# Layer 1's scores of both maps in one five-bank PSUM region

## The chip, the cores and the metric

The kernel runs on one core of a Trainium2 chip. The metric is the time of the whole program on the device, in microseconds (us), as the median of several executions; smaller is better. A profile is one further execution, recorded by the hardware, from which spans of single instructions are read. The engines named are TensorE (PE; its weight loads stand as PEld), VectorE (DVE), ScalarE (ACT), GpSimd (POOL) and SyncE (SP, which only issues DMAs here).

## What is computed

The reference is a two-layer transformer over 1024 latent tokens and 256 context tokens, width 1024. Layer 0 is a multi-head latent attention, layer 1 a differential attention with 8 heads; both end in a gated output projection and a layer norm. The change is in layer 1, which for each head does this (context tokens are keys only, since no later layer needs their output):

```python
# per head h: two maps m of 64-wide queries and keys, one 128-wide value
s1 = q1 @ k1.T * scale          # (1024, 1280): 1024 latent and 256 context keys
s2 = q2 @ k2.T * scale
o  = softmax(s1) @ v - lam * (softmax(s2) @ v)
o  = rms_norm(o, g_sub) * (1 - lambda_init) * silu(gate)
```

Everything is float32 in the reference. The kernel keeps that accuracy by splitting each operand into a high and a low float16 part and adding three products (high x high, high x low, low x high).

## The kernel before

**Steps.** Layer 1 runs over 8 heads and, in each, over 8 tiles of 128 queries: 64 steps. `step1` (L1345) issues one step. In the text below a tile's work is spread over three steps: scores and softmax in step t, the turn of its weights in step t+1, its product with the values in step t+2.

- *Scores* (`scores1`, L1135): for map 0 and 1, matmuls against 1280 keys, two each (L1144 and L1145, high and low query), in pieces of at most 512 columns. Before, every piece goes to a PSUM bank of its own from a rotation of eight: first the 256 context columns of both maps in one bank, then two banks of 512 a map. DVE takes the negated maximum of each bank (L1157, L1161) and combines them (L1163); ACT takes the exponential of each piece and its sum (L1167). After both maps DVE adds the sums up (L1170), inverts them (L1171), forms the factor of map 2 (L1172) and joins the maps (L1173: `p0 + factor * p1`, 1280 wide, from SBUF).
- *Turn* (`turn1`, L1176): PE transposes the joined weights, ten blocks of 128 x 128 (L1180), in groups of 4, 4 and 2, each group in a bank; `split16` (L179) writes the high part with ACT (L181) and the low part with DVE (L182), once a group.
- *Values* (`values1`, L1184): 30 matmuls (L1188 to L1190) into one bank; ACT scales the result out (L1193) and squares it (L1194), POOL makes the norm's factor (L159, L160) and applies it (L1201), and a DMA writes it to `o_d`.
- *Side work*: the projections of the next head's keys, queries, values and gate (`prod_k1`, `prod_q1`, `prod_v1`), and the preparation of their weights (`prod_w`). Projections are matmuls of three products (`mm3`, L185 to L187) over eight blocks of the inner dimension, and come in pieces of 512 columns (keys, queries) or 256 columns (value and gate). Keys and queries get a rotary embedding: DVE shuffles and multiplies (L1048, L1049), POOL multiplies and adds (L1050, L1051), then `split16` writes `kH` and `kL`. Values and gate are copied out by ACT (L1122, L1124), split into `vh` and `vl`, and the gate gets a SiLU (L1129). `prod_w` squares the loaded weights (L979, ACT), makes a scale from them (L982 to L989, PE, DVE and POOL) and splits them into `wH` and `wL`.

**What sets the order.** PE's order is written out by hand: within the loop over heads PE executes in the order in which the program calls it. The orders of ACT, DVE, POOL and SP are set by the framework's scheduler when the program is built, and each engine then works through its list in order. The framework also puts in the waits between engines, from the tiles that instructions write and read. How much side work PE does between the parts of a step is set by `SLOT1`, five numbers in units of PE columns: after map 0's scores (and, before, all of its exponentials are issued), after map 1's scores and the values, and after each group of the turn. In the last head there is no next projection; there the side work is the output projection (`out_tile1`, fp32 matmuls) and the transposes of its input (`out_turn`, L1262), by `SLOTO`.

```python
SLOT1 = 2900, 2900, 2900, 2900, 2900
SLOTO = 0, 7000, 7000, 7000, 7000
```

PSUM has eight banks of 512 fp32 columns. From L1006 on, all eight rotate under one tag (`bank("b")`): scores, turns, values, projections and output.

Of the kernel before, what the change touches and what calls it, by code (L numbers as in the profile page):

```python
# [9 lines left out]
F32 = mybir.dt.float32  # L10
# [3 lines left out]
AF = mybir.ActivationFunctionType  # L14
ALU = mybir.AluOpType
AX = mybir.AxisListType

P = 128
D = 1024
KT = D // P  # L20
SEQ = 1024
CTX = 256
NTOK = SEQ + CTX
NT = NTOK // P
# [16 lines left out]
CHUNKS = ((0, 512), (512, 512), (1024, 256))  # L41
MROW0, MROW1 = 16.0, 1024.0
PW = 16.0
SLOT1 = 2900, 2900, 2900, 2900, 2900
SLOTO = 0, 7000, 7000, 7000, 7000
SWAP16 = [(i + 16) % 32 for i in range(32)]

# [1 line left out]
def fv(ap):  # L49
    return ap.bitcast(F32)  # L50
# [3 lines left out]
def hybrid_kernel(  # L54
# [7 lines left out]
    pe, act, dve, pool, sp = nc.tensor, nc.scalar, nc.vector, nc.gpsimd, nc.sync  # L62
# [6 lines left out]
    def nm(s):  # L69
        uid[0] += 1  # L70
        return f"{s}_{uid[0]}"
# [3 lines left out]
    banks = {}  # L75
    pstack = ctx.enter_context(ExitStack())

    def set_banks(**tags):
        pstack.close()
        banks.clear()  # L80
        banks.update(tags)
        banks["pool"] = pstack.enter_context(
            tc.tile_pool(name=nm("psum"), bufs=1, space=bass.MemoryType.PSUM, reuse_waits="tile"))
# [4 lines left out]
    def bank(tag, dt=F32):  # L88
        return banks["pool"].tile([P, 512], dt, tag=tag, bufs=banks[tag], name=nm("ps_" + tag))
# [21 lines left out]
    def col(n, name, dt=F32):  # L111
        return cpool.tile([P, n], dt, tag=name, name=name)
# [21 lines left out]
    lcf = col(3, "lcf")  # L134
# [15 lines left out]
    idn = fv(idr)  # L150
# [24 lines left out]
    def split(hi, lo, src, e_hi=None, e_lo=None):  # L175
        (e_hi or act.copy)(hi, src)
        (e_lo or dve).tensor_tensor(lo, src, fv(hi), op=ALU.subtract)  # L177

    def split16(hi, lo, src, scale):  # L179

        act.activation(hi, src, AF.Copy, scale=scale)  # L181
        dve.scalar_tensor_tensor(lo, src, scale, hi, op0=ALU.mult, op1=ALU.subtract)  # L182
# [628 lines left out]
    def chain(*gs):  # L811
        for g in gs:
            yield from g
# [72 lines left out]
    with ow_ctx, spool("o0") as op0:  # L886
# [14 lines left out]
        for t in (8, 9, 0, 1, 2, 3, 4, 5, 6, 7):  # L901
# [5 lines left out]
            s = 0 if t < 8 else 1  # L907
# [7 lines left out]
            for hh in range(2):  # L915
                tb = bank("d")
# [40 lines left out]
    def w1(tag):  # L957
        sh, d, b = TAG1[tag]
        return rot(place[tag], sh, d, tag, b)
# [43 lines left out]

    for _ in prod_w(0, 0, lambda: bank("c"), act):
        pass
    set_banks(b=8)  # L1006

    sp.dma_start(cosB, cs1[0])
    sp.dma_start(sinB, cs1[1])
# [125 lines left out]
    def scores1(h, t):  # L1135

        ks = kt1[h]
        q1, qs = qt1[h]
        ts = slice(t * P, (t + 1) * P)
        mx, sm = w1("mx"), w1("sm")  # L1140
        p = [w1("p0"), w1("p1")]

        def st_of(out, m, c0, n):
            pe.matmul(out, qs[m][:, ts], ks[m][:, c0:c0 + n], start=True, stop=False)  # L1144
            pe.matmul(out, q1[m][:, ts], ks[m][:, c0:c0 + n], start=False, stop=True)  # L1145

        st = {}

        def chunk(c0, ms):
            n = 512 // len(ms)  # L1150
            st[c0, ms] = b = bank("b")
            for i, m in enumerate(ms):
                st_of(b[:, i * n:(i + 1) * n], m, c0, n)
            return b

        b = chunk(SEQ, (0, 1))
        dve.tensor_reduce(mx[:, 0:2], b.rearrange("p (a b) -> p a b", a=2), axis=AX.X, op=ALU.max, negate=True)  # L1157
        for m in range(2):
            for i, c0 in enumerate((0, 512)):
                b = chunk(c0, (m,))  # L1160
                dve.tensor_reduce(mx[:, 2 + 2 * m + i:3 + 2 * m + i], b, axis=AX.X, op=ALU.max, negate=True)  # L1161
            nb = mx[:, 6 + m:7 + m]
            dve.tensor_scalar(nb, mx[:, 2 * m + 2:2 * m + 3], mx[:, 2 * m + 3:2 * m + 4], mx[:, m:m + 1],  # L1163
                              op0=ALU.min, op1=ALU.min)
            for i, (c0, n, b) in enumerate(((0, 512, st[0, (m,)]), (512, 512, st[512, (m,)]),
                                            (SEQ, CTX, st[SEQ, (0, 1)][:, m * CTX:(m + 1) * CTX]))):
                act.activation(p[m][:, c0:c0 + n], b, AF.Exp, bias=nb,  # L1167
                               accum_out=sm[:, 2 + 3 * m + i:3 + 3 * m + i])
            yield
        dve.tensor_reduce(sm[:, 0:2], sm[:, 2:8].rearrange("p (a b) -> p a b", a=2), axis=AX.X, op=ALU.add)  # L1170
        dve.reciprocal(sm[:, 2:4], sm[:, 0:2])  # L1171
        dve.scalar_tensor_tensor(sm[:, 4:5], sm[:, 3:4], nlam, sm[:, 0:1], op0=ALU.mult, op1=ALU.mult)  # L1172
        dve.scalar_tensor_tensor(p[0], p[1], sm[:, 4:5], p[0], op0=ALU.mult, op1=ALU.add)  # L1173
        yield p[0], sm

    def turn1(pc, ph, pl, k0, n):  # L1176

        st = bank("b")
        for j in range(n):
            pe.transpose(st[:, j * P:(j + 1) * P], pc[:, (k0 + j) * P:(k0 + j + 1) * P], idn)  # L1180
        split16(ph[:, k0:k0 + n, :], pl[:, k0:k0 + n, :],
                st[:, :n * P].rearrange("p (a b) -> p a b", a=n), lcf[:, 0:1])

    def values1(h, t, ph, pl, sm):  # L1184
        vh, vl = vt[h]
# [76 lines left out]
    def out_turn(t, k0, n):  # L1262

        o, _ = og[t]
        if k0 == 0:
            oT[t] = w1("tH"), w1("tL")
        tH, tL = oT[t]
        tb = bank("b")
        for j in range(n):
            pe.transpose(tb[:, j * P:(j + 1) * P], o[:, (k0 + j) * P:(k0 + j + 1) * P], idn)  # L1270
        f = lambda x: x[:, k0:k0 + n, :].rearrange("p a b -> p (a b)")
        split(f(tH), f(tL), tb[:, :n * P])
# [65 lines left out]
    with tc.manual_schedule(engines={ENG[c] for c in MAN1}):  # L1338
        for _ in chain(weave(chain(prod_k1(0), prod_q1(0, 0), prod_q1(0, 1)), prod_w(0, 1), WAT[0]),
                       weave(prod_v1(0), prod_w(1, 0), WAT[1])):  # L1340
            while later:
                later.pop(0)()
        joined, turned = [], []

        def step1(cur, side, at):  # L1345

            with tc.high_priority(HP):
                if cur:
                    S = scores1(*cur)
                    next(S)  # L1350
            some(side, at[0])
            with tc.high_priority(HP):
                if cur:
                    next(S)
                if turned:
                    values1(*turned.pop(0))
            some(side, at[1])
            pc = None
            if joined:
                c_, pc, sm = joined.pop(0)  # L1360
                ph, pl = w1("ph"), w1("pl")
                turned.append((*c_, ph, pl, sm))
            for (k0, n), v in zip(((0, 4), (4, 4), (8, 2)), at[2:]):
                if pc is not None:
                    with tc.high_priority(HP):
                        turn1(pc, ph, pl, k0, n)
                some(side, v)
            if cur:
                with tc.high_priority(HP):
                    joined.append((cur, *next(S)))  # L1370
            for _ in range(len(later)):
                later.pop(0)()

        g1 = gate_row1()
        part = lambda: (v for _, v in zip(range(4), g1))
        for h in range(H1):
            last = h == H1 - 1
            if not last:
                G = chain(weave(weave(chain(prod_k1(h + 1), prod_q1(h + 1, 0), prod_q1(h + 1, 1)), part(), (1, 9, 17, 25)),
                                prod_w(h + 1, 1), WAT[0]),  # L1380
                          weave(prod_v1(h + 1), prod_w(h + 2, 0) if h + 2 < H1 else
                                chain(*[out_w1(k, lambda: w1("ws").rearrange("p a b -> p (a b)")) for k in range(NOW)]),
                                WAT[1] if h + 2 < H1 else range(1, 40, 4)))
            else:
                while later:
# [96 lines left out]
```

## Time and profile before

| | us |
|---|---|
| median of 3 runs | 1862.71 |
| lowest and highest run | 1861.32 and 1863.7 |
| the profiled execution (span from first to last instruction) | 1870.0 |
| PE busy in it | 1696.2 |
| DVE busy | 1245.6 |
| ACT busy | 1077.1 |
| POOL busy | 835.2 |

The profiled execution is 0.4% longer than the median of the runs. The mean clock granted to TensorE in it was 0.969 of full speed. Busy time is the union of an engine's rows; a PE row reaches from a matmul's start to the modelled end of its results, and the next matmul can start before that end. In a row of the groups, the first numbers after the bar are total busy time and mean nanoseconds of one instruction; the number after the second bar is the time for which its engine stood idle just before such an instruction, followed by what ended that idling. In a row of the waits: total us, times, longest. In a row of the timeline: start, length, engine, line, operation. In a row of the stretches: bounds, length, then busy us with counts for PE, PEld, DVE, ACT and POOL, the granted clock, the DMA share and GB/s.

Layer 1's steps run from about 1032 us to the end.

### The profile page before, as it was taken

To read this page: it belongs to the slowest core of one execution; us is meant where nothing else is said; L and a number is where in the kernel's file an instruction comes from. 1 tells how busy PE (TensorE), PEld (TensorE's weight loads), DVE (VectorE), ACT (ScalarE), POOL (GpSimd) and SP (SyncE) were. 2 spreads that over 40 slices of the span, in tenths; PEclk is the share of its full clock that TensorE was granted. 3 is DMA by queue.
4 is the path that set the end of the run, shared out by engine and by line. 5 is a ranking of instruction groups with operands and counts; after the bars stand their busy time and mean duration, and the time that the engine had idled before them with its cause. 6 is when DMAs were issued, how large, how long until landed. Compare 5 with 4: busy or idle time off the path is not lost. (4 is left out here: it accounts for less than half of the span.)

```text
span 1870.0 us, 36547 instructions
## 1 busy us (share of the span) xinstructions
PE 1696.2 (91%) x14468; PEld 1237.0 (66%) x14468; DVE 1245.6 (67%) x2072; ACT 1077.1 (58%) x2143; POOL 835.2 (45%) x741
## 2 busy tenths in 40 slices
PE   7889998999999998868979999999999999988998
PEld 3888965656666565556756576767666666666776
DVE  7546766565565657526764777787877777878674
ACT  3432047867777787711123667676767676767542
POOL 1443026767767676646662213222222222433654
PEclk9999799999999999979999999999999999999999
DMA  8245630111111113043333222222121212224341
GB/s 307 62 126 182 189 108 18 39 33 36 42 44 32 32 41 100 25 164 123 124 127 106 71 63 66 62 64 58 56 49 44 59 46 61 63 53 139 99 131 68
DMA packets 111225, 154.84 MB, mean 83 GB/s; under 512 B 13415, under 2 KB 84679, under 8 KB 111054
## 3 DMA queue, kind: packets, MB, share of 16 engines
q1 hardware_dynamic: 104238, 146.22, 26.1%
q10 hardware_dynamic: 6816, 6.29, 1.0%
q8 instruction: 114, 1.87, 0.4%
q14 instruction: 57, 0.47, 0.1%
HBM read 98.65 MB, written 27.07 MB: 67 GB/s over the span
## 5 line engine op out<-in xcount | busy, mean ns | idle before, releaser
L716 POOL TENSOR_TENSOR pl<-p,ph 128x1024 f16<-128x1024 f32 (+1 forms) x176 | 362.8, 2066 | 155.9 <-ACT ph L715 129.5
L1167 ACT ACTIVATE p<-ps_b,mx 128x512 f32<-128x512 f32 (+1 forms) x384 | 230.6, 618 | 83.1 <-DVE mx L1163 82.7
L696 DVE TENSOR_REDUCE mx<-ps_a 128x1 f32<-128x1024 f32 x128 | 155.6, 1223 | 138.2 <-PE ps_a L694 138.2
L714 ACT ACTIVATE p<-ps_a,esc 128x1024 f32<-128x1024 f32 (+1 forms) x176 | 189.2, 1075 | 100.4 <-PE ps_a L772 94.5
L715 ACT CAST ph<-p 128x1024 f16<-128x1024 f32 (+1 forms) x176 | 177.1, 1006 | 5.5
L1161 DVE TENSOR_REDUCE mx<-ps_b 128x1 f32<-128x512 f32 x256 | 165.6, 682 | 0.0
L785 PE MATMUL ps_d<-Vh,pl 128*128 128x65 f16 x1344 | 147.5, 195 | 5.2 <-POOL pl L716 5.1
L782 PE MATMUL ps_d<-Vh,ph 128*128 128x65 f16 x1344 | 149.5, 196 | 0.0
L784 PE MATMUL ps_d<-Vl,ph 128*128 128x64 f16 x1344 | 148.3, 193 | 0.0
L185 PE MATMUL ps_b<-h1H,wH 128*128 128x512 f16 (+1 forms) x384 | 133.5, 348 | 14.1 <-DVE pl L182 6.7
L185 PE MATMUL ps_b<-wH,h1H 128*128 128x256 f16 x512 | 139.5, 272 | 4.4 <-ACT p L1167 4.2
L1192 POOL TENSOR_TENSOR sm<-sm,us 128x1 f32<-128x1 f32 x64 | 18.3, 285 | 271.9 <-DVE sm L1171 258.6
L187 PE MATMUL ps_b<-wH,h1L 128*128 128x256 f16 x512 | 139.5, 273 | 0.0
L186 PE MATMUL ps_b<-wL,h1H 128*128 128x256 f16 x512 | 139.5, 272 | 0.0
L1144 PE MATMUL ps_b<-KS,QS 128*128 128x512 f16 (+1 forms) x384 | 126.1, 345 | 12.0 <-DVE pl L182 6.1
L782 PEld LDWEIGHTS <-ph 128*128 128x128 f16 x1344 | 124.2, 98 | 18.4 <-issue 5.5
L187 PE MATMUL ps_b<-h1H,wL 128*128 128x512 f16 (+1 forms) x384 | 133.2, 347 | 0.8 <-DVE wL L182 0.8
L186 PE MATMUL ps_b<-h1L,wH 128*128 128x512 f16 (+1 forms) x384 | 133.4, 347 | 0.0
L784 PEld LDWEIGHTS <-ph 128*128 128x128 f16 x1344 | 124.9, 99 | 12.4 <-issue 0.8
L770 PE MATMUL ps_a<-qH,KH 100*128 100x512 f16 x320 | 123.6, 386 | 9.7 <-ACT p L714 4.3
L1145 PE MATMUL ps_b<-KS,Q 128*128 128x512 f16 (+1 forms) x384 | 129.1, 345 | 0.0
L785 PEld LDWEIGHTS <-pl 128*128 128x128 f16 x1344 | 124.1, 98 | 6.6 <-POOL pl L716 6.5
(370 smaller groups left out, 5161.9 us busy)
## 6 DMA issues: line engine op xcount, KB each, us to landing
ws<-in_dw SPq DMA_DIRECT2D x30, 512.0 KB, 3.8
adw<-in_ada_w SPq DMA_DIRECT2D x24, 512.0 KB, 5.0
g<-sg_d SPq DMA_DIRECT2D x18, 512.0 KB, 3.7
adaw<-in_ada_w SPq DMA_DIRECT2D x16, 512.0 KB, 7.1
sg_d<-gg ACTq DMA_DIRECT2D x40, 128.0 KB, 2.8
o<-o_d SPq DMA_DIRECT2D x10, 512.0 KB, 3.5
o_d<-op SPq DMA_DIRECT2D x7, 640.0 KB, 3.7
xt<-in_xT SPq DMA_DIRECT2D x16, 256.0 KB, 3.6
```

The costliest lines, as they stand in the source:

```text
L185: pe.matmul(ps, aH, bH, start=start, stop=False, skip_group_check=skip)
L186: pe.matmul(ps, aH, bL, start=False, stop=False, skip_group_check=skip)
L187: pe.matmul(ps, aL, bH, start=False, stop=stop, skip_group_check=skip)
L696: dve.tensor_reduce(mx[:, t, 0:1], ps, axis=AX.X, op=ALU.max)
L714: act.activation(p32[:, :n], st, AF.Exp, scale=esc0)
L715: act.copy(ph[:, :n], p32[:, :n])
L716: pool.tensor_tensor(pl[:, :n], p32[:, :n], ph[:, :n], op=ALU.subtract)
L782: pe.matmul(pv[:, t, :], ph[:, ts], Vh[:, k, h, :], start=(k == kcs[0] and t == 0), stop=False, skip_group_check=True)
L784: pe.matmul(pv[:, t, :V0], ph[:, ts], Vl[:, k, h, :], start=False, stop=False, skip_group_check=True)
L785: pe.matmul(pv[:, t, :], pl[:, ts], Vh[:, k, h, :], start=False, stop=(k == NT - 1), skip_group_check=True)
L1161: dve.tensor_reduce(mx[:, 2 + 2 * m + i:3 + 2 * m + i], b, axis=AX.X, op=ALU.max, negate=True)
L1167: act.activation(p[m][:, c0:c0 + n], b, AF.Exp, bias=nb, accum_out=sm[:, 2 + 3 * m + i:3 + 3 * m + i])
```

## The change

Five of the eight banks become one tile, `spsum`, of 2 x 1280 fp32 columns, allocated once; three banks are left in the rotation. Map 0's scores stand in columns 0 to 1279 (banks 0, 1 and half of 2), map 1's in columns 1280 to 2559. Each map then has one maximum (L1157 of the changed kernel) and one exponential with its sum (L1158), both 1280 wide; the combining and adding instructions go. The first 256 columns of map 1 are computed right after map 0. The turn writes its ten transposes to columns 0 to 1279 of the same tile, in groups of 8 and 2 (L1177), and splits them with one pair of 1280-wide instructions. In the last head, the output's first seven transposes go to columns 1536 on (L1267). The slots of side work become `2900, 0, 2900, 4350, 4350`; their sum is as before. Scores are at L1145 and L1146, values at L1185 to L1187 in the changed kernel.

```diff
-SLOT1 = 2900, 2900, 2900, 2900, 2900
+SLOT1 = 2900, 0, 2900, 4350, 4350
...
-    set_banks(b=8)
+    set_banks(b=3)
+    spsum = banks["pool"].tile([P, 2 * NTOK], F32, tag="s", bufs=1, name=nm("ps_s"))
...
-        b = chunk(SEQ, (0, 1))
-        dve.tensor_reduce(mx[:, 0:2], b.rearrange("p (a b) -> p a b", a=2), axis=AX.X, op=ALU.max, negate=True)
-        for m in range(2):
-            for i, c0 in enumerate((0, 512)):
-                b = chunk(c0, (m,))
-                dve.tensor_reduce(mx[:, 2 + 2 * m + i:3 + 2 * m + i], b, axis=AX.X, op=ALU.max, negate=True)
-            nb = mx[:, 6 + m:7 + m]
-            dve.tensor_scalar(nb, mx[:, 2 * m + 2:2 * m + 3], mx[:, 2 * m + 3:2 * m + 4], mx[:, m:m + 1],
-                              op0=ALU.min, op1=ALU.min)
-            for i, (c0, n, b) in enumerate(((0, 512, st[0, (m,)]), (512, 512, st[512, (m,)]),
-                                            (SEQ, CTX, st[SEQ, (0, 1)][:, m * CTX:(m + 1) * CTX]))):
-                act.activation(p[m][:, c0:c0 + n], b, AF.Exp, bias=nb,
-                               accum_out=sm[:, 2 + 3 * m + i:3 + 3 * m + i])
-            yield
-        dve.tensor_reduce(sm[:, 0:2], sm[:, 2:8].rearrange("p (a b) -> p a b", a=2), axis=AX.X, op=ALU.add)
+        W = NTOK
+        cuts = (0, 512, 1024, W), (0, 256, 768, W)
+
+        def part(m, i):
+            c0, c1 = cuts[m][i:i + 2]
+            st_of(spsum[:, m * W + c0:m * W + c1], m, c0, c1 - c0)
+
+        def weights(m):
+            s_ = spsum[:, m * W:(m + 1) * W]
+            dve.tensor_reduce(mx[:, m:m + 1], s_, axis=AX.X, op=ALU.max, negate=True)
+            act.activation(p[m], s_, AF.Exp, bias=mx[:, m:m + 1], accum_out=sm[:, m:m + 1])
+
+        for i in range(3):
+            part(0, i)
+        part(1, 0)
+        weights(0)
+        yield
+        for i in (1, 2):
+            part(1, i)
+        weights(1)
+        yield
...
-        st = bank("b")
-        for j in range(n):
-            pe.transpose(st[:, j * P:(j + 1) * P], pc[:, (k0 + j) * P:(k0 + j + 1) * P], idn)
-        split16(ph[:, k0:k0 + n, :], pl[:, k0:k0 + n, :],
-                st[:, :n * P].rearrange("p (a b) -> p a b", a=n), lcf[:, 0:1])
+        for j in range(k0, k0 + n):
+            pe.transpose(spsum[:, j * P:(j + 1) * P], pc[:, j * P:(j + 1) * P], idn)
+        if k0 + n == NT:
+            split16(ph, pl, spsum[:, :NTOK].rearrange("p (a b) -> p a b", a=NT), lcf[:, 0:1])
...
-        tb = bank("b")
+        tb = spsum[:, 1536 + k0 * P:] if n > 1 else bank("b")
...
-            for (k0, n), v in zip(((0, 4), (4, 4), (8, 2)), at[2:]):
-                if pc is not None:
+            for (k0, n), v in zip(((0, 8), (8, 2), (NT, 0)), at[2:]):
+                if pc is not None and n:
```

More of the change, by code (lines that the diff above doesn't have):

```diff
@@ L1145, in st_of @@
             pe.matmul(out, q1[m][:, ts], ks[m][:, c0:c0 + n], start=False, stop=True)
[L1147 to L1154, printed above, removed]
-        b = chunk(SEQ, (0, 1))
-        dve.tensor_reduce(mx[:, 0:2], b.rearrange("p (a b) -> p a b", a=2), axis=AX.X, op=ALU.max, negate=True)
-        for m in range(2):
-            for i, c0 in enumerate((0, 512)):
-                b = chunk(c0, (m,))
-                dve.tensor_reduce(mx[:, 2 + 2 * m + i:3 + 2 * m + i], b, axis=AX.X, op=ALU.max, negate=True)
-            nb = mx[:, 6 + m:7 + m]
-            dve.tensor_scalar(nb, mx[:, 2 * m + 2:2 * m + 3], mx[:, 2 * m + 3:2 * m + 4], mx[:, m:m + 1],
-                              op0=ALU.min, op1=ALU.min)
-            for i, (c0, n, b) in enumerate(((0, 512, st[0, (m,)]), (512, 512, st[512, (m,)]),
-                                            (SEQ, CTX, st[SEQ, (0, 1)][:, m * CTX:(m + 1) * CTX]))):
-                act.activation(p[m][:, c0:c0 + n], b, AF.Exp, bias=nb,
-                               accum_out=sm[:, 2 + 3 * m + i:3 + 3 * m + i])
-            yield
-        dve.tensor_reduce(sm[:, 0:2], sm[:, 2:8].rearrange("p (a b) -> p a b", a=2), axis=AX.X, op=ALU.add)
+        W = NTOK
[16 more added lines that the diff above has]
+        yield
         dve.reciprocal(sm[:, 2:4], sm[:, 0:2])
```

## The prediction

> **What bounds the kernel now.** I read the page first (busy shares and the 40 slices), then the timeline of DVE for the length of a head of layer 1, the timeline of PE for what a step costs, and the waits.
>
> ```profile
> span 1870.0 us, 36547 instructions
> PE 1696.2 (91%) x14468; PEld 1237.0 (66%) x14468; DVE 1245.6 (67%) x2072; ACT 1077.1 (58%) x2143; POOL 835.2 (45%) x741
> ...
> PE   7889998999999998868979999999999999988998
> ```
>
> PE is the bound, at 9 tenths or more through nearly all of layer 1 (slices 22 to 40). The change touches layer 1 alone, so what counts is what makes PE wait there. Layer 1 goes by heads of 8 steps (one query tile each); the first reduction of a head marks its start:
>
> ```profile
> 1033.33 0.69 DVE L1157 TENSOR_REDUCE mx<-ps_b 128x2 f32<-128x512 f32 x1 [0.73 <-PE ps_b L1145]
> ...
> 1706.28 0.68 DVE L1157 TENSOR_REDUCE mx<-ps_b 128x2 f32<-128x512 f32 x1
> ```
>
> These are head 0 and head 7: (1706.28 - 1033.33) / 7 = 96.1 us a head. How much of it is PE's own work? PE overlaps its rows, so I take distances between starts.
>
> ```profile
> 1395.84 0.22 PE L1190 MATMUL ps_b<-vh,pl 128*128 128x128 f16 x1
> 1395.90 0.22 PE L1188 MATMUL ps_b<-vh,ph 128*128 128x128 f16 x1
> ...
> 1398.06 0.60 PE L1180 MATMUL ps_b<-idr,p 128*128 128x128 f32 x4
> ...
> 1404.43 0.27 PE L1144 MATMUL ps_b<-KS,QS 128*128 128x256 f16 x1
> ...
> 1404.54 0.27 PE L1145 MATMUL ps_b<-KS,Q 128*128 128x256 f16 x1
> ...
> 1404.87 0.38 PE L1144 MATMUL ps_b<-KS,QS 128*128 128x512 f16 x1
> ...
> 1405.08 0.38 PE L1145 MATMUL ps_b<-KS,Q 128*128 128x512 f16 x1
> ```
>
> 512 columns cost 0.21 us, 256 cost 0.11, a value matmul 0.055, a transpose (0.60 - 0.27) / 3 = 0.11: some 0.417 us per 1000 columns. A head has 8 x 5120 columns of scores (17.1 us), 8 x 30 value matmuls (13.2), 80 transposes (8.8) and, counted from the loops, 110,592 columns of projections (46.2): 85.3 us. So **10.8 us a head, 1.35 a step, is all that PE loses to waits today**; across seven heads a perfect change could win 76 us. The largest such wait is for the exponentials:
>
> ```profile
> PE ps_b L1180 <- ACT p L1167: 16.3, 19, 2.0
> ```
>
> That is 16.3 us in 19 waits, in the stretch of the seven heads.
>
> **The change part by part.** PE's matmuls are the same in number and size; they are only reordered. ACT and DVE get fewer, longer instructions. What decides is what PE waits for. In the changed program as built, the waits on the region `ps_s` are by the whole tile, not by the columns: map 1's second chunk (columns 1536 on) waits for map 0's exponential (columns 0 to 1279) in 64 of 64 steps; the first transpose (columns 0 on) waits for map 1's exponential in 62 of 64; map 1's maximum waits for map 0's exponential; the next step's first score waits for the low half of the split. In before, scores went to fresh banks of eight. So a step becomes one chain: scores 0, maximum, exponential, scores 1, maximum, exponential, transposes, split high, split low, next scores. PE works through it only with what its hand-written order has between.
>
> No row of before is 1280 wide from PSUM; I extend the nearest rows in a straight line.
>
> ```profile
> L1161 DVE TENSOR_REDUCE mx<-ps_b 128x1 f32<-128x512 f32 x256 | 165.6, 682 | 0.0
> L696 DVE TENSOR_REDUCE mx<-ps_a 128x1 f32<-128x1024 f32 x128 | 155.6, 1223 | 138.2 <-PE ps_a L694 138.2
> ...
> L182 DVE SCALAR_TENSOR_TENSOR pl<-ps_b,lcf,ph 128x512 f16<-128x512 f32 x128 | 90.8, 744 | 13.4 <-ACT ph L181 13.4
> ...
> L182 DVE SCALAR_TENSOR_TENSOR pl<-ps_b,lcf,ph 128x256 f16<-128x256 f32 x64 | 30.4, 476 | 1.4 <-ACT ph L181 1.4
> ```
> ```profile
> L714 ACT ACTIVATE p<-ps_a,esc 128x1024 f32<-128x1024 f32 x160 | 178.3, 1114 | 100.4 <-PE ps_a L772 94.5 <-PE ps_a L705 5.9
> L1167 ACT ACTIVATE p<-ps_b,mx 128x512 f32<-128x512 f32 x256 | 173.4, 686 | 83.1 <-DVE mx L1163 82.7
> ...
> L181 ACT ACTIVATE ph<-ps_b,lcf 128x512 f16<-128x512 f32 x128 | 88.5, 715 | 13.1 <-PE ps_b L1180 13.1
> ...
> L181 ACT ACTIVATE ph<-ps_b,lcf 128x256 f16<-128x256 f32 x64 | 32.7, 511 | 2.7 <-PE ps_b L1180 2.7
> ```
>
> Maximum: 0.682 + 768 x (1.223 - 0.682) / 512 = 1.49. Exponential: 0.686 + 768 x (1.114 - 0.686) / 512 = 1.33. Split high: 0.715 + 768 x (0.715 - 0.511) / 256 = 1.33; low: 0.744 + 768 x (0.744 - 0.476) / 256 = 1.55. Bounds: no less than the 1024-wide 1.22 and 1.11, no more than two and a half 512-wide ones, 1.71 and 1.72. The straight line is nearest. The hand-overs:
>
> ```profile
> 420.46 0.59 PE L694 MATMUL ps_a<-KH,qH 96*128 96x512 f16 x2
> ...
> 421.10 2.36 DVE L696 TENSOR_REDUCE mx<-ps_a 128x1 f32<-128x1024 f32 x2 [0.50 <-PE ps_a L694]
> ```
> ```profile
> 1409.08 0.27 DVE L1163 TENSOR_SCALAR mx<-mx 128x1 f32<-128x1 f32 x1
> ...
> 1409.38 0.69 ACT L1167 ACTIVATE p<-ps_b,mx 128x512 f32<-128x512 f32 x1 [1.05 <-DVE mx L1163]
> ```
> ```profile
> 1399.82 0.67 ACT L1167 ACTIVATE p<-ps_b,mx 128x512 f32<-128x512 f32 x1
> ...
> 1400.38 0.19 ACT L1167 ACTIVATION_READ_ACCUMULATOR p<-ps_b,mx 128x1 f32 x1
> ...
> 1400.63 0.27 PE L185 MATMUL ps_b<-wH,h1H 128*128 128x256 f16 x1 [0.34 <-ACT p L1167]
> ```
>
> PE to DVE 0.05, DVE to ACT 0.03, the accumulator read 0.08 past the exponential, ACT to PE 0.06; a matmul ends 0.16 after the next could start. Maximum and exponential together: 0.16 + 0.05 + 1.49 + 0.03 + 1.33 + 0.08 + 0.06 = **3.2 us**, twice a step.
>
> *Wait 1* (map 0): the cover is the side work at slot 2900, two pieces of 1536 columns, 1.28 us; PE stands 1.92. *Wait 2* (map 1): slot 0 gives no side work, 30 value matmuls cover 1.65; PE stands 1.55. *Wait 3* (split, 1.33 + 1.55 + 0.3 = 3.2 too): 3.2 to 3.8 us of side work covers it in seven steps, 2.56 in the eighth: 0.6 a head. A clean head: 85.3 + 8 x 3.47 + 0.6 = 113.7, that is 17.6 over today; seven heads **+123 us**.
>
> *Queues.* On ACT and DVE, whose order is fixed, other work stands ahead of a link of this chain; it now holds PE up directly.
>
> ```profile
> L181 ACT ACTIVATE wH<-ws,uw 128x1024 f16<-128x1024 f32 x30 | 32.9, 1138 | 23.4 <-DVE uw L286 23.4
> ...
> L979 ACT ACTIVATE wsq<-ws 128x1024 f32<-128x1024 f32 x27 | 29.1, 1080 | 19.2 <-DMA ws<-in_dw 19.2
> ...
> L181 ACT ACTIVATE kH<-rr,es 128x512 f16<-128x512 f32 x16 | 11.7, 732 | 32.6 <-POOL rr L1051 32.6
> L181 ACT ACTIVATE vh<-Vf,kc 128x1280 f16<-128x1280 f32 x8 | 11.3, 1407 | 0.0
> ...
> L1129 ACT ACT_TABLE_LOAD x8 | 10.3, 1283 | 0.1
> ...
> L1129 ACT ACTIVATE gg<-gg,uw 128x1024 f32<-128x1024 f32 x8 | 9.2, 1150 | 0.1
> ```
> ```profile
> L1050 POOL TENSOR_TENSOR rsw<-rsw,sinB 128x512 f32<-128x512 f32 x30 | 38.1, 1270 | 86.7 <-DVE rsw L1048 86.7
> ```
>
> From the changed order, per head, against an exponential that could start 3.0 us into its step: step 0 has vh, silu and two table loads first (1.41 + 1.15 + 2 x 1.28 = 5.1 us from 0.4 on): 2.5 late. Step 2: the maximum stands behind a scalar that waits for two rope passes on POOL (2 x 1.27) and the weight-range chain, 2.5 late, then two wH and kH ahead of map 1's exponential, 0.9. Steps 3 and 4: kH waits for the rope on POOL (3.5 us in, then 0.73), in step 3 a 1.08 square after it: 2.5 and 1.2. Step 6: two wH (1.1), two squares ahead of the split (0.9). Sum 11.6 a head, **+81 us**. Bounds: 0, if order and idle gaps hide all; 120, if each comes half again longer. ACT's saving (six exponentials and three splits become two and one) is off PE's path. So are the smaller maxima. Three banks for the rest cost nothing here: a bank's reader has finished two allocations earlier, covered by the matmuls between.
>
> *Last head.* Slot 0 is 0, so wait 1 is bare: 3.2 instead of 1.92. Slot 1 (7000 columns) covers wait 2. The output transposes now write the same tile and so wait for the split: 3.2 less 0.64 of cover, 2.6. How long such a step takes today:
>
> ```profile
> 1785.57 0.64 DVE L1157 TENSOR_REDUCE mx<-ps_b 128x2 f32<-128x512 f32 x1
> ...
> 1802.55 0.64 DVE L1157 TENSOR_REDUCE mx<-ps_b 128x2 f32<-128x512 f32 x1
> ```
>
> That is 16.98 us, against 15.95 of matmuls by the distances above: 1.0 lost. Six full steps x (3.2 + 2.6 - 1.0) is 29; with the two short first steps I take **+31**.
>
> Sum: 1870 + 123 + 81 + 31 + 10 (clock, below) = 2115 in a profiled execution. The three runs' median is 1862.71 against the 1870.0 of this one, 0.4% less: **2107 us**.
>
> **Rules weighed.** What a wait does to the clock, the trace of before shows once in full:
>
> ```profile
> 1174.35 0.44 PE L1180 MATMUL ps_b<-idr,p 128*128 128x128 f32 x2 [1.96 <-ACT p L1167]
> ```
> ```profile
> 1172.00:1176.00 4.00, 2.04 (x14) 1.38 (x13) 4.00 (x9) 2.48 (x9) 0.00 (x0) 0.93 0.48 110
> 1176.00:1180.00 4.00, 4.00 (x21) 2.49 (x20) 3.05 (x8) 3.26 (x10) 2.73 (x3) 0.65 0.46 136
> ```
>
> After 1.96 us of idling the granted clock sinks to 0.93 and 0.65 of full speed in two stretches of 4 us: 4 x 0.07 + 4 x 0.35 = 1.7 us of PE's work are lost. I charge 0.5 us for each of some 20 long waits (the late steps above), since a slow stretch falls partly into the next wait: the 10 us. The Trainium skill (TensorE: Matmul & The Clock Gate, section What's actually happening) has the gate fall to half after an idle window of about 3.4 us; the row above fell after less, and by the rule the sum would be the same, as only the late steps stand that long.
>
> **Rivals.** (a) *Clean chain*: the same waits, but the queue delays vanish into the engines' new idle time: 1870 + 123 + 31 = 2024, 2016 timed. For it: ACT and DVE lose work. Against: the order is fixed. (b) *Clock*: every step's two stands trip the gate, 1.7 us lost in each of 56 steps, +95: 2210, 2201 timed. For it: the row above; against: both stands are shorter than 2 us in a clean step. (c) *Faster, by bank*: the waits bind only where both sides touch one bank of 512 columns. Then wait 1 is gone (bank 3 against 0 to 2), and of wait 2 only the last two transposes (bank 2) wait, 0.5 us: map 1's maximum starts 4.5 us into the step, its exponential ends at 7.7, PE comes at 7.2. A head is 85.3 + 4 + 0.6 = 89.9, seven win 43: 1827, 1820 timed. It decides where the two stands together fall under today's 1.35 us a step, against 3.47 worked out. Against: the program's waits are tile-wide in every step. The Trainium skill (PSUM — Partial Sum Buffer, section PSUM bank collisions raise a hardware error) asks for guards by bank and quadrant, no wider, which is what (c) would be; no run here shows a collision. (d) The change doing nothing: excluded, the waits are in the program.
>
> **How the numbers follow.** Forecast 0.62, (a) 0.19, (b) 0.13, (c) 0.04, rest 0.02. Upper end: 2107, and 39 for the queue delays at their upper bound, and 34, half of what the 1280-wide pairs at their upper bound would add (112 x 0.61): 2180. Lower end: (a), 2016, less a fifth of what their lower bound would take off (112 x 0.49): 2005. (b), (c) and the rest stay out, 0.19. A measurement of this kernel tells about 0.2% from no change. Faster 0.04, within 0.2% 0.01, slower 0.95.
>
> **What would show it.** Right: heads of 120 to 130 us; in the waits, PE's second map (line 1145) standing for ACT's exponential some 2 us in each of 64 steps, and the transposes (1177) for it some 1.5; DVE and ACT under 60% busy in layer 1; 1280-wide rows near 1.5 and 1.3. Wrong: PE 90% busy in layer 1, waits under 1.35 us a step, or granted clock near 0.8 throughout (rival b).

## The result

The changed kernel takes **2179.09 us** (median of 4 runs, 2175.37 to 2184.89), the one before 1862.01 beside it (4 runs, 1860.17 to 1863.7): a ratio of 1.1703, 95% interval 1.168 to 1.1726. It is 317 us slower. The forecast was 2107, its range 2005 to 2180: the sign and the mechanism held. The time lies at the range's very top, and two of the four runs (2180.25 and 2184.89) lie above it.

**The profile after.** The head of the page, and its slices:

```profile
span 2173.6 us, 35376 instructions
...
PE 1778.5 (82%) x14468; PEld 1293.1 (59%) x14468; DVE 1199.3 (55%) x1560; ACT 1011.5 (47%) x1503; POOL 888.3 (41%) x741
...
PE   7989999999999869879667777777877777776777
...
PEclk9998999999999989989899899999999999998889
```

The number of matmuls is the same, 14468. DVE and ACT have lost 46 and 66 us of work, and PE, at 9 tenths through layer 1 before, is now at 6 to 8. Its busy time has grown by 82 us, though it does the same work: most of that is the granted clock, as the stretches below show. In what follows PE "stands" while it sits idle before an instruction that waits. Where did the 303.6 us between the two profiled executions arise? The stretches of layer 1, first of before, then of after: seven heads, then the last one with the end.

```profile
1033.33:1706.28 672.95, 624.80 (x5242) 451.88 (x5241) 521.61 (x1020) 460.72 (x1264) 191.21 (x311) 0.99 0.21 56
1706.28:1870.00 163.72, 142.30 (x927) 112.77 (x925) 108.29 (x197) 78.55 (x192) 82.72 (x79) 0.95 0.37 124
```
```profile
1030.25:1939.63 909.38, 683.47 (x5238) 491.86 (x5237) 479.02 (x575) 405.36 (x707) 242.79 (x311) 0.92 0.15 41
1939.63:2173.60 233.97, 168.87 (x926) 129.54 (x925) 108.49 (x130) 68.75 (x109) 87.74 (x79) 0.84 0.27 86
```

Length less PE's busy time is PE's idle time. The seven heads: 909.38 - 672.95 = 236.4 longer, of which 177.8 is idle (48.1 became 225.9) and 58.7 is busy time at a granted clock of 0.92 instead of 0.99. The last head: 70.3 longer, 43.7 idle and 26.6 busy, clock 0.84 for 0.95. So nearly three quarters of the loss is standing, the rest longer busy time. PE's waits in the seven heads name all of the standing (their sum is 225.5):

```profile
PE ps_s L1145 <- ACT p L1158: 162.9, 56, 8.7
PE ps_s L1177 <- ACT p L1158: 58.8, 48, 3.1
PE ps_s L1145 <- DVE pl L182: 3.8, 8, 0.5
```

These are the prediction's three waits: map 1's scores for map 0's exponential (wait 1), the transposes for map 1's (wait 2), the next scores for the split (wait 3). One after the other on PE's timeline they look so; the bracket holds the idle time just before the row:

```profile
1305.61 0.59 PE L1145 MATMUL ps_s<-KS,QS 128*128 128x512 f16 x1 [3.72 <-ACT p L1158]
...
1310.58 1.09 PE L1177 MATMUL ps_s<-idr,p 128*128 128x128 f32 x8 [0.88 <-ACT p L1158]
...
1321.41 0.38 PE L1145 MATMUL ps_s<-KS,QS 128*128 128x512 f16 x1 [1.74 <-ACT p L1158]
...
1325.53 1.09 PE L1177 MATMUL ps_s<-idr,p 128*128 128x128 f32 x8 [1.43 <-ACT p L1158]
...
1338.46 0.38 PE L1145 MATMUL ps_s<-KS,QS 128*128 128x512 f16 x1 [4.31 <-ACT p L1158]
```

A clean step stands for 1.74 and 1.43 us; step 0 (3.72) and step 2 (4.31) are late. What the clock makes of the matmuls behind the stands of 1.74 and 4.31 is in two stretches of 4 us that begin with them:

```profile
1321.41:1325.41 4.00, 2.69 (x34) 2.04 (x33) 1.49 (x1) 1.35 (x3) 0.00 (x0) 1.00 0.00 0
1338.46:1342.46 4.00, 4.00 (x33) 3.44 (x33) 2.75 (x3) 4.00 (x4) 0.00 (x0) 0.60 0.00 0
```

Almost the same 33 or 34 matmuls take 2.69 us at full clock behind the clean wait, and all 4 us at 0.60 behind the late one. The rows show the same behind step 0, whose first matmul takes 0.59 us for 0.38, and why wait 2 is only 0.88 there: the matmuls that cover it are slower, so PE arrives later. Part of what the clock takes falls into the next wait.

### The profile page after: what moved, and what is told of

It is laid out like the page before. It is cut to its first block, busy times and chain, and to the rows that moved or that the text cites. A ratio compares the mean times of both kernels' runs of the same rounds, so it can differ in the third digit from the quotient of the medians.

```text
span 2173.6 us, 35376 instructions
## 1 busy us (share of the span) xinstructions
PE 1778.5 (82%) x14468; PEld 1293.1 (59%) x14468; DVE 1199.3 (55%) x1560; ACT 1011.5 (47%) x1503; POOL 888.3 (41%) x741
## 4 chain that ended last, share of the span: by engine, by line
PE 48%; DVE 17%; ACT 15%; issue 7%; DMA 6%; POOL 5%; SPq 1%; DVEq 0%; POOLq 0%; ACTq 0%
PE ps_b L187 5%; PE ps_b L185 5%; ACT p L1158 5%; PE ps_b L186 5%; DVE mx L1157 5%; PE ps_s L1177 4%; PE ps_a L770 3%; PE ps_s L1145 3%; PE ps_a L771 2%; PE ps_a L772 2%; DMA ws<-in_dw 2%; PE ps_s L1146 2%; ACT ph L181 2%; PE ps_a L185 2%; DVE pl L182 2%
## 5 line engine op out<-in xcount | busy, mean ns | idle before, releaser
L1157 DVE TENSOR_REDUCE mx<-ps_s 128x1 f32<-128x1280 f32 x128 | 190.7, 1490 | 226.5 <-PE ps_s L1146 226.5
L1158 ACT ACTIVATE p<-ps_s,mx 128x1280 f32<-128x1280 f32 x128 | 169.4, 1323 | 295.8 <-DVE mx L1157 295.7
L1145 PE MATMUL ps_s<-KS,QS 128*128 128x512 f16 (+1 forms) x384 | 140.4, 374 | 203.7 <-ACT p L1158 191.5
L1146 PEld LDWEIGHTS <-Q 128*128 128x128 f16 x384 | 39.0, 102 | 250.3 <-issue 227.1
L182 DVE SCALAR_TENSOR_TENSOR pl<-ps_s,lcf,ph 128x1280 f16<-128x1280 f32 x64 | 99.2, 1550 | 131.2 <-ACT ph L181 131.2
L1185 PE MATMUL ps_b<-vh,ph 128*128 128x128 f16 x640 | 150.4, 260 | 0.0
L1186 PE MATMUL ps_b<-vl,ph 128*128 128x128 f16 x640 | 149.7, 260 | 0.0
L1187 PE MATMUL ps_b<-vh,pl 128*128 128x128 f16 x640 | 148.8, 259 | 0.0
L181 ACT ACTIVATE ph<-ps_s,lcf 128x1280 f16<-128x1280 f32 x64 | 85.0, 1329 | 133.4 <-PE ps_s L1177 133.4
L1177 PE MATMUL ps_s<-idr,p 128*128 128x128 f32 x640 | 96.9, 284 | 60.9 <-ACT p L1158 60.6
```

Source lines behind the costliest of these rows:

```text
L1157: dve.tensor_reduce(mx[:, m:m + 1], s_, axis=AX.X, op=ALU.max, negate=True)
L1158: act.activation(p[m], s_, AF.Exp, bias=mx[:, m:m + 1], accum_out=sm[:, m:m + 1])
L1177: pe.transpose(spsum[:, j * P:(j + 1) * P], pc[:, j * P:(j + 1) * P], idn)
L1185: pe.matmul(ps, ph[:, kc, :], vh[:, kc, :], start=kc == 0, stop=False)
```

## The experiments

Ratios are against runs of the kernel before on the same chip, with 95% intervals. The theory: PE stands because one tile holds both maps and the turn, so that whole-tile waits put maximum, exponential, maximum, exponential and split in one chain; queues on ACT and DVE lengthen it, and the clock adds to it. The rivals: the order of side work, the shortage of banks, or the clock alone.

**1. More cover in the same chain.** Only the slots of the changed kernel are altered.

```diff
-SLOT1 = 2900, 0, 2900, 4350, 4350
+SLOT1 = 6000, 3000, 0, 2750, 2750
```

> The changed kernel with the side work dealt out otherwise: slots 6000, 3000, 0, 2750, 2750 in place of 2900, 0, 2900, 4350, 4350. Theory (PE stands for the tile-wide waits, less what side work covers): wait 1 falls from 1.92 to 0.64 us a step, wait 2 from 1.55 to 0.3, wait 3 rises from 0 to 1.0; 1.5 us a step less, some 85 us in seven heads, and fewer falls of the clock: 2060 to 2095 us. Rival (the time is lost to work queued ahead on ACT and DVE, whatever PE does meanwhile): 2165 to 2195.

Measured: 2054.93, ratio 1.1029 (1.1002 to 1.1057), 124 us less and 5 below the theory's range. The waits of layer 1, last head included:

```profile
PE ps_s L1145 <- ACT p L1158: 97.9, 63, 7.5
PE ps_s L1145 <- DVE pl L182: 66.2, 56, 9.2
...
PE ps_s L1177 <- ACT p L1158: 8.7, 10, 1.8
```

Wait 1 is halved, wait 2 nearly gone, and wait 3 has come up in their place, since the split has 5500 columns behind it instead of 8700. The same side work hides what it stands in front of; there is too little of it for all three.

**2. A tile for each map.** Three banks each, two left for the rest; maximum, exponential and split stay 1280 wide, and the slots stay those of the changed kernel. The turn writes map 0's tile, the output's turns map 1's.

```diff
-    set_banks(b=3)
-    spsum = banks["pool"].tile([P, 2 * NTOK], F32, tag="s", bufs=1, name=nm("ps_s"))
+    set_banks(b=2)
+    smap = [banks["pool"].tile([P, 1536], F32, tag=f"s{m}", bufs=1, name=nm(f"ps_s{m}")) for m in range(2)]
...
-            s_ = spsum[:, m * W:(m + 1) * W]
+            s_ = smap[m][:, :W]
...
-            pe.transpose(spsum[:, j * P:(j + 1) * P], pc[:, j * P:(j + 1) * P], idn)
+            pe.transpose(smap[0][:, j * P:(j + 1) * P], pc[:, j * P:(j + 1) * P], idn)
```

> The changed kernel with a three-bank tile for each map, so that no wait goes across the maps; two banks are left for the rest, map 1's columns are cut 256, 512, 512 as before, and the output's eighth transpose goes to map 1's tile too. All 1280-wide instructions stay. Theory (the waits across the maps are the loss): waits 1 and 2 go in all steps, 56 x 3.47 = 194 us and 35 in the last head, and with them most of the clock's falls, some 75: 1850 to 1900 us. Rival (too few banks for the rest, or the wide instructions): with one bank fewer still, 2150 or more.

Measured: 1941.34, ratio 1.0433 (1.0396 to 1.047). Of 317 us, 238 are gone, with the wide instructions all in place; 77 us stay, more than the theory said. The run also has six banks for the maps instead of five and two for the rest instead of three, so 238 is what is left after those.

```profile
PE ps_s L1145 <- DVE pl L182: 23.3, 19, 4.0
...
PE ps_s L1177 <- ACT p L1158: 18.3, 17, 2.5
PE ps_b L185 <- ACT gg L1125: 17.0, 17, 1.2
PE ps_b L1185 <- DVE kr L1063: 10.8, 7, 1.6
```

Wait 1 is gone; waits on the rest's two banks (`ps_b`) are new, 47 us in sum. Two more runs kept these tiles and dealt the side work out anew: slots of 4000, 0, 0, 5250, 5250 and of 5000, 1500, 0, 4000, 4000.

> A tile of three banks for each map and two banks for the rest, as in the run with two tiles, and besides the slots 4000, 0, 0, 5250, 5250: more cover ahead of the transposes for map 0's exponential, the ten transposes together, 10500 columns behind the split. That run took 1941. Theory (what was left there are the waits of the transposes and of the next scores on queue delays, some 66 us in the waits, beside some 35 for the shortage of two banks): 1890 to 1920 us. Rival (the rest is the two banks, or the clock): 1935 us or more.

> Two tiles of three banks again, with the slots 5000, 1500, 0, 4000, 4000: 5.4 us of matmuls between map 0's scores and the transposes, 3.3 behind them for the split. With the slots 2900, 0, 2900, 4350, 4350 it took 1941, with 4000, 0, 0, 5250, 5250 1961. Theory (what is left are the transposes' waits for map 0's exponential, some 40 to 70 us of idling): 1900 to 1925 us. Rival (two banks for the rest are the bound, so that moved side work only moves the waits): 1935 us or more.

Measured: 1961.12, ratio 1.0522 (1.0503 to 1.0542), and 1943.19, ratio 1.0428 (1.0403 to 1.0453). Both missed the theory and lie where the rival put them, at 1935 or more. In the first, the transposes' wait for ACT's exponential grew from 18.3 to 32.5 us in spite of more cover; why is open. In the second it nearly went (3.3 us), and wait 3 grew instead:

```profile
PE ps_s L1145 <- DVE pl L182: 45.5, 29, 4.0
```

The waits on the rest's two banks were as before, 47 us in sum. The 77 us did not go with either set of slots; no run gave these two tiles a third bank for the rest.

**3. Wait 2 alone.** As in 2, but the turn goes to map 1's tile (`smap[1]` for `smap[0]` in the turn and its split).

> A tile of three banks for each map as in the run with two tiles, and the slots of the changed kernel, but the turn goes to map 1's tile instead of map 0's: the transposes wait for map 1's exponential again (wait 2), no score waits for the other map's (wait 1 gone), and the split has the next scores of map 0 and a slot of side work in front of the next writer. That run took 1941. Theory (wait 2 costs by itself: some 1.4 us a step bare in 56 steps, and queue delays of map 1's pair): 2000 to 2050 us. Rival (wait 1 is the whole loss; wait 2 only repeats it): 1935 to 1965.

Measured: 2070.67, ratio 1.1116 (1.1095 to 1.1137): 129 us more than in 2, where the theory said 60 to 110. The two runs differ in nothing but the tile that the turn writes.

```profile
PE ps_s L1177 <- ACT p L1158: 135.7, 57, 5.9
```

That is 2.4 us a step, not the clean 1.43 and not the 1.2 that wait 2 has in the changed kernel (58.8 / 48). Wait 2 by itself costs more than half of what all the waits across maps do (129 of 238), so the waits do not add up: where one is taken away, another becomes longer. That it meets the queues which wait 1 took on itself before is likely, but no run shows it alone.

**4. Single banks: five, or six, for scores and turns.** The kernel before with its 512-column pieces, its scores and turns restricted to five banks (the rest has three), then to six (the rest has two). The output's turns are among the five or six too, except in the first the eighth.

```diff
-    set_banks(b=8)
+    set_banks(s=5, b=3)
...
-            st[c0, ms] = b = bank("b")
+            st[c0, ms] = b = bank("s")
...
-        st = bank("b")
+        st = bank("s")
```

> The kernel before, with its 512-wide instructions and its order, but with the banks divided as in the change: scores, turns and output transposes rotate in five banks, all else in three. Theory (the division of the banks costs next to nothing): 1855 to 1880 us. Rival (three banks left for the rest cost a good part of the 317 us): 1920 or more.

> The kernel before with single banks of 512 columns, six of them for scores, turns and the output's turns and two for the rest (the run with five and three took 1925). Theory (that run's loss is the turn's first bank, which is that of the context scores and comes free only with map 1's last exponential; a sixth bank gives an earlier one): 1880 to 1910 us. Rival (the loss is the shortage in the rest's banks): above 1925.

Measured: 1924.89, ratio 1.0332 (1.0307 to 1.0356), and 1937.54, ratio 1.0401 (1.0382 to 1.0421). Both went against the theory and lie in the ranges of the rivals; the waits say whether for the rivals' reasons. With five and three:

```profile
PE ps_s L1180 <- ACT p L1167: 71.2, 34, 5.6
...
PE ps_b L185 <- ACT gg L1124: 6.1, 7, 0.9
```

With six and two:

```profile
PE ps_b L1120 <- ACT gg L1124: 17.4, 7, 2.5
PE ps_b L185 <- ACT gg L1124: 16.8, 9, 2.6
PE ps_s L1180 <- ACT p L1167: 16.1, 15, 2.1
PE ps_b L185 <- ACT o L1193: 13.5, 12, 1.8
...
PE ps_b L1188 <- DVE uw L286: 7.3, 6, 2.0
PE ps_b L185 <- DVE kr L1049: 5.7, 5, 1.4
```

The sixth bank does what was expected of it: the transposes' wait falls from 71.2 to 16.1, the size that it had in before. But the third bank, taken from the rest, costs as much: the five waits on `ps_b` shown come to 60.7, against the 6.1 above (with the smaller ones 69 against 8). So three banks for the rest are nearly free and two are not, and five for scores and turns, rotated in the order of the kernel before, are too few even when each bank is waited for by itself. The first run's rival had the number right and the banks wrong; the second's had both right.

**5. The order of side work alone.** The kernel before, eight banks, with the changed kernel's slots; and the other way, with 4000, 4000, 2500, 2000, 2000.

> The kernel before with only the slots of the changed one (2900, 0, 2900, 4350, 4350 for five times 2900), eight banks as before. Theory (the order of side work alone costs little while scores go to fresh banks; the waits are the region's): 1855 to 1890 us. Rival (the order alone, with no side work between map 1's scores and the transposes, is a large part of the loss): 1920 us or more.

> The kernel before with only its slots changed, to 4000, 4000, 2500, 2000, 2000: the other way from the changed kernel's slots, which alone cost 23 us. Theory (side work ahead of the transposes hides the exponentials): the waits of the transposes shrink by up to 16 us, 1848 to 1862 us. Rival (moved side work is missed behind the turn as much as it helps before it): 1863 to 1885.

Measured: 1886.32, ratio 1.012 (1.01 to 1.014), and 1864.5, ratio 1.0005 (0.9989 to 1.0021). The new order costs 23 us by itself, in the upper part of the theory's range. The other way makes no difference: that theory failed, and there is nothing to win from the slots of before.

**6. One queue.** The changed kernel without the gate's SiLU, so that ACT does not change its function table twice in step 0 of a head.

```diff
-            act.activation(g, g, AF.Silu, scale=uv)
+            act.activation(g, g, AF.Copy, scale=uv)
```

> The changed kernel with the gate's SiLU left out (a plain scaled copy stands in its place), so that ACT no longer swaps its function table twice a head in step 0; all else as after. Theory (queues on ACT ahead of the chain hold PE up): step 0's wait for map 0's exponential falls from 3.7 to about 1.7 us, 2 to 4 us a head with the clock, so 2150 to 2165 us. Rival (what stands ahead of the exponential is not what makes step 0 late): 2175 to 2185.

Measured: 2164.1, ratio 1.1617 (1.1583 to 1.1652), 15 us less. Step 0 and step 2 of the head whose steps are shown above, in this kernel:

```profile
1295.89 0.38 PE L1145 MATMUL ps_s<-KS,QS 128*128 128x512 f16 x1 [1.74 <-ACT p L1158]
...
1327.89 0.59 PE L1145 MATMUL ps_s<-KS,QS 128*128 128x512 f16 x1 [4.31 <-ACT p L1158]
```

Step 0's 3.72 has become the clean 1.74, and step 2's 4.31 has stayed. The exponentials that ended the two stands of step 0, first with the SiLU and then without:

```profile
1304.14 1.33 ACT L1158 ACTIVATE p<-ps_s,mx 128x1280 f32<-128x1280 f32 x1
```
```profile
1294.42 1.33 ACT L1158 ACTIVATE p<-ps_s,mx 128x1280 f32<-128x1280 f32 x1 [0.75 <-DVE mx L1157]
```

In both kernels PE goes on 1.47 us after this instruction starts. With the SiLU ACT came to it from a table load without a pause; without it ACT had been idle for 0.75 us and waited for the maximum. So what stands in ACT's queue ahead of the exponential holds PE up. For step 2 the trace of the changed kernel names DVE's queue: its maximum comes behind an instruction that waits for POOL.

```profile
1335.40 0.15 DVE L284 TENSOR_SCALAR uw<-uw 128x1 int32<-128x1 int32 x1 [3.02 <-POOL uw L986]
1335.47 1.48 DVE L1157 TENSOR_REDUCE mx<-ps_s 128x1 f32<-128x1280 f32 x1
```

**7. The clock.** The changed kernel with matmuls of 384 columns, into columns that nobody reads, in front of wait 1 (10, and 18 in the last head) and behind the values (8), so that PE is not seen idle.

```diff
+    def fill(h, ph, n):
+        vh = vt[h][0]
+        for _ in range(n):
+            pe.matmul(vbank[0][:, P:512], ph[:, 0, :], vh[:, 0:3, :], start=True, stop=True)
...
+            if cur and turned:
+                vbank.append(bank("b"))
+                fill(turned[0][0], turned[0][2], FILL[0] if at is SLOT1 else FILL[2])
...
+        fill(h, ph, FILL[1])
```

> The changed kernel with idle matmuls of 384 columns (0.16 us each) into unused columns of the values' bank: 10 ahead of wait 1 (18 in the last head) and 8 ahead of wait 2, so that PE works in its stands instead of idling. They add no result. Theory now (the clock's falls cost 60 to 80 us, where the prediction charged 10): they run in time that is lost anyway, the granted clock in layer 1 rises from 0.92 to over 0.97, and the time falls to 2100 to 2140 us. Rival 1 (the clock costs about 10): 2165 to 2185. Rival 2 (PE does not stand there): up by 64 x 2.9 = 185, over 2300.

Measured: 2155.2, ratio 1.1571 (1.1535 to 1.1607), 24 us less. Its seven heads:

```profile
1022.75:1918.60 895.85, 802.31 (x6212) 555.43 (x6211) 479.86 (x575) 408.80 (x707) 233.12 (x311) 0.98 0.16 42
```

The clock is up from 0.92 to 0.98 and the heads are shorter by 13.5 us: matmuls that compute nothing of use shorten the run. Neither number that was on record holds: the clock is worth more than 10 us, and removing most of its loss gained less than 60 to 80. A likely reason is that faster matmuls cover less, so that PE stands longer for the same chain; no run shows it alone. The fill can hold PE up a little itself, so 24 is more likely too low than too high.

**8. The last head.** The changed kernel with the last head's side work placed anew.

```diff
-SLOTO = 0, 7000, 7000, 7000, 7000
+SLOTO = 3500, 3500, 0, 7000, 14000
...
-        tb = spsum[:, 1536 + k0 * P:] if n > 1 else bank("b")
+        tb = spsum[:, 1536 + k0 * P:]
```

> The changed kernel with only the last head's side work placed anew (SLOTO 3500, 3500, 0, 7000, 14000 for 0, 7000, 7000, 7000, 7000; the output's eighth transpose goes to the region too): 3500 columns now lie ahead of map 1's rest, the transposes follow at once and the output's transposes come later after the split. Theory (the last head's 70 us over before are bare waits of 3.5 us for map 0's exponential, of 2.4 us for the split, and the clock that these take): the waits shrink to some 1.9 and under 1, the last head with the tail falls from 234 to 180 to 200, so 2125 to 2150 us. Rival (the last head is long for another reason, such as the output projection on three banks): 2170 us or more.

Measured: 2154.37, ratio 1.1569 (1.1546 to 1.1593), 25 us less, between the two. Its last head:

```profile
1937.60:2150.00 212.40, 155.55 (x926) 115.13 (x925) 112.08 (x130) 67.85 (x109) 90.40 (x79) 0.92 0.29 95
```

It is 21.6 us shorter than in the changed kernel, of which 13.3 is busy time at a clock of 0.92 instead of 0.84, and 8.2 idle. Covering the waits brought back under a third of the 70 us. What the other 49 are was not taken apart further; PE's named waits there still sum to 48 us, against 13 in before.

No version was faster than the kernel before.

## Why the prediction was right, and where it was short

**Right: what waits, and how long a clean link is.** The waits are whole-tile, as read from the changed program, and a head takes 909.38 / 7 = 129.9 us, where 120 to 130 was named as the sign; DVE and ACT are busy for 53% and 45% of the seven heads. The 1280-wide durations, in a straight line from 512 and 1024 (1.49, 1.33, 1.33, 1.55 us), against the groups of after:

```profile
L1157 DVE TENSOR_REDUCE mx<-ps_s 128x1 f32<-128x1280 f32 x128 | 190.7, 1490 | 226.5 <-PE ps_s L1146 226.5
L1158 ACT ACTIVATE p<-ps_s,mx 128x1280 f32<-128x1280 f32 x128 | 169.4, 1323 | 295.8 <-DVE mx L1157 295.7
...
L182 DVE SCALAR_TENSOR_TENSOR pl<-ps_s,lcf,ph 128x1280 f16<-128x1280 f32 x64 | 99.2, 1550 | 131.2 <-ACT ph L181 131.2
...
L181 ACT ACTIVATE ph<-ps_s,lcf 128x1280 f16<-128x1280 f32 x64 | 85.0, 1329 | 133.4 <-PE ps_s L1177 133.4
```

They came out to 0.01 us. So did the clean links: 1.92 for wait 1 is 1.74 of idling and the 0.16 of the last matmul's end; 1.55 for wait 2 is 1.43 and the same; wait 3 is 3.8 in sum for 4.2. The clean chain's +123 stands. The experiments with two tiles show that the waits across maps are the cause: 238 of 317 us go with them, and 129 come back when the turn alone makes one of them again.

**Too large: the queues.** Forecast +81 in seven heads. In idle time, 56 x (1.74 + 1.43) = 177.5 of the 225.5 is the clean chain and 3.8 is wait 3; 44 are left. Wait 1 is late by 162.9 - 56 x 1.74 = 65.5 us, 9.4 a head for 11.6, but wait 2 is shorter by 56 x 1.43 - 58.8 = 21.3. The mechanism is shown by experiment for step 0, late by 2.0 us for 2.5 forecast, and by the trace for step 2, 2.6 for 2.5 (both in 6); the other steps were not taken apart. The step that failed is the adding up: what wait 1 loses, wait 2 gets back in part, once by the slow clock under its cover.

**Too small: the clock.** This step failed: "0.5 us for each of some 20 long waits", 10 us. PE's busy time shows 58.7 more in seven heads and 26.6 more in the last, 85.3 in sum; the matmul ends that now stand ahead of a wait are part of it (some 112 waits x 0.16 = 18 at the most). The text had seen one such loss in before, 1.7 us, and cut it to 0.5 since a slow stretch would fall into the next wait. It does so, but the stretches were more and each cost more: the trace's clock records hold 32 slow stretches in the seven heads, 136.5 us at 0.50, that is 68 us of clock, some of it in PE's idle time; before has two of 3.4 us each in its seven. Nor did the text weigh that in before three other stands of 1.96 us (the matmuls at 1271.17, 1367.34 and 1558.59) left the clock at 1.00. Rival (b), a trip in every step, fell as a mechanism, since the clean step shows a clock of 1.00, but its 95 us were nearer to these 68 than the 10. How much of the time the clock alone decides is not shown more closely than between some 24 us (experiment 7) and 85.

**Too small: the last head.** Forecast +31, measured +70.3. The waits were right in size (3.5 and 2.4 us for 3.2 and 2.6), but these lines, of the whole last head, show more of them than "six full steps":

```profile
PE ps_s L1145 <- ACT p L1158: 28.6, 8, 5.0
PE ps_s L1267 <- DVE pl L182: 16.0, 7, 2.4
PE ps_s L1145 <- DVE pl L182: 8.3, 2, 5.3
```

Eight, seven and two waits make 52.9 us, with two small ones 56.3; before had 12.8 there. The other 26.6 is busy time at the lower clock, which the term had none of. Slow stretches follow both waits, here the shorter one, with the 4 us behind it:

```profile
2045.65 0.97 PE L1267 MATMUL ps_s<-idr,o 128*128 128x128 f32 x4 [2.40 <-DVE pl L182]
```
```profile
2045.65:2049.65 4.00, 4.00 (x15) 3.20 (x16) 0.98 (x2) 0.86 (x2) 0.00 (x0) 0.57 0.15 20
```

**Right, within 6 us: three banks for the rest.** In the changed kernel's seven heads no wait on `ps_b` is listed; in experiment 4 the rest's three banks cost 6.1 us of waits, two 60 and more. What the text did not see is the other side: five banks were too few for scores and turns even with waits by bank (+61 us). That also speaks against rival (c), which had waits by bank at 1820; in its own form, wide instructions with waits by bank, it was not tried, since the framework's waits go by tiles; nor was the one tile with narrow instructions. Rival (a), the clean chain at 2016, fell with experiment 6 and with 44 us of late waits.

If the parts added up, the 317 us would be about 23 for the order (experiment 5), 61 for five banks at all (experiment 4) and some 233 for making one tile of them and wide instructions on it. The 238 of experiment 2 are near that, but this proves little: that run pays for two banks for the rest, and the waits do not add up.

The forecast landed 72 us low. In the profiled execution, 2173.6 stands against the sum of 2115: 59. The last head makes +39 of these, layer 1 begins 3 us earlier, and the seven heads, 236.4 longer for 123 + 81 + 10 = 214, make the other +22. In the heads the queues are 37 too large, so the rest, the clock above all, is some 59 too small; how much of that is the clock alone is open. That the time fell inside the range is in part luck: the queues' excess hid more than half of what the other terms of the heads lacked. The other 13 lie between profile and median: the forecast took 8 off because before's profiled execution was longer than its median, and after's was 5 shorter.

## What to carry to other kernels

A wider instruction is paid for by what its tile holds together: read from the built program which instructions wait for the whole tile, and price the chain that this makes, not the instructions saved (112 us of DVE and ACT work went here, and 317 us came). On an engine in fixed order, count the waits of about two microseconds and more and add the slow clock that can follow each (1.7 us of work for 3.41 us at half, in this trace); it was the largest omission here. And PSUM banks are a currency between stages: a bank given to one is taken from another, and the price can turn round within a single bank.

## What the runs showed of the chip

The length of a stand alone does not decide whether the granted clock falls. Behind a stand of 1.96 us that ended at 1141.05 it was 0.57 over 4 us, behind one of the same length that ended at 1405.15 it was 1.00; stands of 2.40 us were followed by 0.57 (at 2045.65) and by 1.00 (at 2019.65). Two stands of 3.50 us, each with three stretches of 3.41 us around it, show what does:

```profile
2006.48 0.38 PE L1145 MATMUL ps_s<-KS,QS 128*128 128x512 f16 x1 [3.50 <-ACT p L1158]
```
```profile
2001.42:2004.83 3.41, 1.56 (x10) 0.80 (x9) 3.41 (x5) 0.00 (x0) 0.00 (x0) 1.00 0.32 108
2004.83:2008.25 3.42, 1.76 (x21) 1.29 (x21) 0.90 (x3) 2.64 (x3) 1.52 (x4) 1.00 0.11 46
2008.25:2011.66 3.41, 3.41 (x29) 2.94 (x27) 1.89 (x3) 2.08 (x5) 3.33 (x2) 1.00 0.00 0
```
```profile
2057.29 0.58 PE L1145 MATMUL ps_s<-KS,QS 128*128 128x512 f16 x1 [3.50 <-ACT p L1158]
```
```profile
2052.62:2056.03 3.41, 1.17 (x8) 0.61 (x7) 3.28 (x5) 0.21 (x1) 0.04 (x1) 1.00 0.50 139
2056.03:2059.44 3.41, 2.15 (x9) 1.03 (x9) 0.18 (x1) 2.43 (x3) 1.87 (x4) 0.50 0.04 14
2059.44:2062.86 3.42, 3.42 (x30) 3.32 (x28) 1.90 (x3) 1.85 (x4) 3.34 (x2) 0.50 0.00 0
```

All slow stretches of layer 1 in this trace begin and end on one grid of 3.41 us, and the stretches above are cut along it. The first stand is halved by a line of the grid: PE is idle for 1.85 us on one side and 1.66 on the other, and the clock stays full. Of the second, 2.24 us fall into one window, and the next one is at half; there PE is idle for another 1.26 us, and the one after stays at half. Counted over layer 1 of the changed kernel: behind a window at full clock with less than 1.95 us of idling the next was full in 227 of 227 cases, with more than 2.0 us it was at half in 41 of 41, and the six between went both ways. Behind a window at half, less than 0.8 us of idling gave a full one in 44 of 44 cases, more than 0.9 us another at half in 17 of 17. So a stand of 2 us can cost 1.7 us of PE's work and one of 3.5 nothing, by where it falls on the grid. The Trainium skill (TensorE: Matmul & The Clock Gate, section Why this matters for your kernels) advises to keep idle gaps between bursts under some 3 us; here one of 1.96 us was already too long, and one of 3.50 was not.
